# Selective-scan unit: states and output products in one group, B·C products beside the turning of x

## The chip, the cores and the metric

The kernel runs on one core of a Trainium2 chip. The metric is the device time of one execution in microseconds (us), lower is better. Of TensorE two names appear: PE is its matmul stream and PEld its weight loads. DVE is VectorE, ACT is ScalarE, and SP is the engine whose queue issues the DMAs.

## The reference, cut to what matters

One layer of a sequence model on 512 tokens, in float32. A state-space mixer (heads of 64 in 8 groups, state size 128) comes first, then further mixers and projections that the change doesn't touch. The part that matters is the scan:

```python
def step(state, inp):
    xc, ac, bc, cc = inp
    cs = jnp.cumsum(ac, axis=1)
    seg = cs[:, :, None] - cs[:, None, :]
    decay = jnp.exp(jnp.where(mask, seg, -jnp.inf))
    cb = jnp.einsum("blgn,bsgn->blsg", cc, bc)
    y_diag = jnp.einsum("blsg,blsgr,bsgrp->blgrp", cb, decay, xc)          # within the chunk
    y_off = jnp.einsum("blgn,bgrpn,blgr->blgrp", cc, state, jnp.exp(cs))   # from the state
    last = cs[:, -1]
    w_in = jnp.exp(last[:, None] - cs)
    new_state = state * jnp.exp(last)[..., None, None] + jnp.einsum("bsgn,bsgr,bsgrp->bgrpn", bc, w_in, xc)
    return new_state, y_diag + y_off
```

Around it stand the projections z, x, B, C = h @ w_in, a causal convolution with silu on x, B and C, and y = (y + d_skip·x)·silu(z). The kernel may cut the sequence into other chunks than the reference: it uses four chunks of 128 tokens.

## The kernel before

**GEMMs.** The projections are done by `gemm` (L178): 96 matmuls of 512 columns give two PSUM tiles (16 steps kt over the depth, for each two column blocks, and for each of those three products of split operands, L197 to L199). Weights come through `wchunk` (L160): one DMA of 512 KB, then `hi` on ACT (L171) and `lo` on DVE (L172).

**Groups, halves, units.** The loop runs over 8 groups g. A group has a GEMM for B and C, then for u = 0 and u = 1 a GEMM for x and one for z. One scan unit belongs to each half; they are called unit n = 2g + u here, 0 to 15. During the z GEMM of a half, `middle(kt)` puts the unit's steps between the GEMM's steps:

- kt 11, `ssd_pre`: a DMA that spreads the running decays over the partitions (`csr`, L1045, one buffer), eight transposes that turn x (`tp`, L1053), and on DVE `xdt` (L1056) and `xdw` (L1059).
- kt 12, `ssd_decay`: for each chunk on ACT the exponentials `dec` (L1097, L1099) and, but for chunk 0, `cex` (L1104); on DVE their products with `cbm` (L1100) and with C (L1105).
- kt 14, `ssd_states`: three products into `sa` and `sb` (L1073), then `st[0]` copied by ACT (L1079), and `st[1]`, `st[2]` each by a DVE multiply (L1081) of the state before and an add (L1083) of the new part.
- after the GEMM, `ssd_unit`: 28 matmuls with 64-row outputs into `yp`. Part 0 (L1122, 16 of them, within a chunk) reads `dec` and `xdt`; part 1 (L1124, 12 of them) reads `cex` and the state. The chunks run 3, 2, 1, 0 with the two parts in turn, so the first part 1 reads the last state, `st[2]`. Then DVE adds the skip (L1127), scales z (`zr`, L565), makes silu of it with ACT (`zt`, L566, L567) and multiplies (L573).

**B·C.** `bc_late` (L511) turns B (`btp`, L514; ACT copy `btok`, L515) and makes the products B·C (`cbp`, L518; masked by DVE to `cbm`, L520). It runs at kt 11 of the x GEMM of u = 0, a whole GEMM ahead of the unit that uses it. The tiles `tp`, `btp`, `cbp`, `sa`, `sb` share two PSUM buffers.

**Unit 0** has no z GEMM behind it yet: its `bc_late`, `ssd_pre`, `ssd_decay` and `ssd_states` stand at kt 1, 5, 6 and 9 of the x GEMM of u = 1. **Unit 15** is the last; after it PE goes on with the output projection, whose operand `ya` (ACT L596, DVE L597) is made of earlier outputs `y`, read back by DMA as `yst` (L606).

**What sets the order.** A scheduler gives each engine its instructions in one fixed order at build time; each engine then runs in that order and waits where an operand isn't there. `issue_after` keeps the 28 matmuls of a unit in their order. GEMM matmuls that don't depend on the unit can stand between them where the scheduler thinks it fit: seven do in unit 8 and ten in unit 15.

Of the kernel before, what the change touches and what calls it, by code (L numbers as in the profile page):

```python
# [13 lines left out]
P = 128  # L14
# [126 lines left out]
class _K:  # L141
    def __init__(self, tc, I, O, dbg):
        self.tc, self.nc, self.I, self.O, self.dbg = tc, tc.nc, I, O, dbg
        self.n = 0

    def nm(self, s):
        self.n += 1
# [30 lines left out]
    def gemm(self, chunks, acts, ncol=2, nk=4, tag=0, before=None, early=True, after=None):  # L178
        nc = self.nc
        ps = [self.pg.tile([P, S], F32, tag=f"g{j + tag}", name=self.nm("g")) for j in range(ncol)]  # L180
        self.mms = []
        nkt = len(chunks) * nk
        kt = 0
        width = ncol * P
        for src in chunks:
            if before:
                before(kt)
            hl = self.wchunk(src, width * nk, early=early)
            for k in range(nk):
                if after:  # L190
                    after(kt)
                a = acts[kt]
                hi, lo = hl[k * 2 // nk]
                for j in range(ncol):
                    o = k % (nk // 2) * width + j * P
                    c = slice(o, o + P)
                    nc.tensor.matmul(ps[j], hi[:, c], a[:, 0, :], start=kt == 0, stop=False)  # L197
                    nc.tensor.matmul(ps[j], hi[:, c], a[:, 1, :], start=False, stop=False)  # L198
                    mm = nc.tensor.matmul(ps[j], lo[:, c], a[:, 0, :], start=False, stop=kt == nkt - 1)  # L199
                    self.mms.append(mm.ins)  # L200
                kt += 1
        assert kt == nkt
        return ps
# [158 lines left out]
    def part1(self):  # L362
# [138 lines left out]
        for g in range(NG):  # L501

            ps = self.gemm(blk(g, 0), hn, after=middle) if g else ps_bc0
            prs = (None, None) if g else pr_bc0
            bt = self.conv_silu(ps[0], 32 + g, tmp.tile([P, S], F32, tag="B", name=f"B{g}", bufs=1), prs[0])
            ct = self.conv_silu(ps[1], 40 + g, tmp.tile([P, S], F32, tag="C", name=f"C{g}", bufs=1), prs[1])
            flush()
            btok = tmp.tile([P, 3, P], F32, tag="btok", name=f"btok{g}", bufs=1)
            cbm = tmp.tile([P, NC, P], F32, tag="cbm", name=f"cbm{g}", bufs=1)

            def bc_late(g=g, bt=bt, ct=ct, btok=btok, cbm=cbm):  # L511
                btp = self.pa.tile([P, NC, P], F32, tag="a", name=f"btp{g}")
                for c in range(3):
                    nc.tensor.transpose(btp[:, c, :], bt[:, c * P : c * P + P], self.ckc("ident"))  # L514
                nc.scalar.activation(btok, btp[:, 0:3, :], AF.Copy)  # L515
                cbp = self.pa.tile([P, NC, P], F32, tag="a", name=f"cbp{g}")
                for c in range(NC):
                    nc.tensor.matmul(cbp[:, c, :], bt[:, c * P : c * P + P], ct[:, c * P : c * P + P],  # L518
                                     start=True, stop=True)
                nc.vector.tensor_tensor(cbm, cbp, self.ckc("triu").unsqueeze(1).to_broadcast([P, NC, P]), ALU.mult)  # L520

            slow = None
            if g:
                mid[11] = [bc_late]
                self.ada(2)
            else:
                mid[11] = [dt_late]
            for u in range(2):  # L530
                if g == 0 and u == 1:
                    mid.update(slow)
                ps = self.gemm(blk(g, 1 + u), hn, after=middle) if g or u else ps_x0
                xs = []
                for j in range(2):
                    xs.append(self.conv_silu(ps[j], g * 4 + u * 2 + j,
                                             tmp.tile([P, S], F32, tag="xs", name=self.nm("xs"), bufs=4)))
                flush()
# [9 lines left out]
                steps = [lambda g=g, u=u, xs=xs, pre=pre: self.ssd_pre(g, u, xs, pre),  # L548
                         lambda g=g, u=u, ct=ct, cbm=cbm, pre=pre: self.ssd_decay(g, u, ct, cbm, pre),
                         lambda g=g, u=u, btok=btok, pre=pre: self.ssd_states(g, u, btok, pre)]  # L550
                unit = lambda g=g, u=u, xs=xs, pre=pre, yy=yg: self.ssd_unit(g, u, xs, pre, yy)
                if g or u:
                    mid.update({11: steps[0:1], 12: steps[1:2], 14: steps[2:3]})
                    late.append(unit)
                else:
                    slow = {1: [bc_late], 5: steps[0:1], 6: steps[1:2], 9: steps[2:3]}
                if g:
                    self.ada(3)
                ps = self.gemm(blk(g, 3 + u), hn, after=middle)
                flush()  # L560
                ths = []
                for j in range(2):
                    th = tmp.tile([P, S], F32, tag="th", name=self.nm("zt"))
                    zr = tmp.tile([P, S], F32, tag="pr", name=self.nm("zr"))
                    nc.vector.tensor_tensor(zr, ps[j], self.rb0, ALU.mult)  # L565
                    nc.scalar.activation(th, zr, AF.Tanh, scale=0.5)  # L566
                    nc.vector.scalar_tensor_tensor(th, th, 1.0, zr, ALU.add, ALU.mult)  # L567
                    ths.append(th)

                def gated(n=len(ys), yg=yg, ths=ths):  # L570
                    for j in range(2):
                        y = yg[j]
                        nc.vector.scalar_tensor_tensor(y, ths[j], 0.5, y, ALU.mult, ALU.mult)  # L573
                        self.sumsq(y)
                        if n + j < 16:
# [489 lines left out]
    def ssd_states(self, g, u, btok, pre):  # L1065
# [4 lines left out]
        sb = self.pa.tile([P, 1, 4, 64], F32, tag="a", name=self.nm("sb"))  # L1070
        parts = [sa[:, 0], sa[:, 1], sb[:, 0]]
        for c in range(3):
            nc.tensor.matmul(parts[c].rearrange("p h d -> p (h d)"), btok[:, c, :],  # L1073
                             xdw[:, c].rearrange("p h d -> p (h d)"), start=True, stop=True)
# [12 lines left out]

    def ssd_decay(self, g, u, ct, cbm, pre):
# [18 lines left out]
        pre.update(decs=decs, cexs=cexs)  # L1107


    def ssd_unit(self, g, u, xs, pre, yg):  # L1110
        nc, tc = self.nc, self.tc
        xdt, st = pre["xdt"], pre["st"]
        yp = [self.py.tile([P, S], F32, tag="y", name=self.nm("yp")) for _ in range(2)]
        prev = None
        for c in (3, 2, 1, 0):
            cl = slice(c * P, c * P + P)
            for part in range(2 if c else 1):
                for h in range(4):
                    o = yp[h // 2][64 * (h % 2) : 64 * (h % 2) + 64, cl]
                    with tc.issue_after(prev) if prev is not None else nullcontext():  # L1120
                        if part == 0:
                            mm = nc.tensor.matmul(o, xdt[:, c, h, :], pre["decs"][c][:, h, :], start=True, stop=c == 0)  # L1122
                        else:
                            mm = nc.tensor.matmul(o, st[c - 1][:, h, :], pre["cexs"][c][:, h, :], start=False, stop=True)  # L1124
# [51 lines left out]
```

## Time and profile before

| | us |
|---|---|
| median of three runs | 2075.62 (2073.63 to 2075.88) |
| the profiled execution, own time | 2072.95 |
| its span, first to last instruction | 2071.2 |
| PE busy | 2049.6 (99%) |
| DVE busy | 1310.7 (63%) |
| ACT busy | 946.2 (46%) |

The mean granted TensorE clock was 0.998 of full speed. The profile is of one execution: the time of a row is when an instruction started on its engine, behind it how long it took, and a note in brackets is idle time ahead of it with what ended it. A row with xN is N instructions in a run. Starts of PE's matmuls are the better measure there, since they are pipelined and their ends are modelled.

### The profile page before, as it was taken

Reading aid. Unit: us, or ns where it says so; the run is one execution under the profiler, and the core shown is the slowest. Engines: PE = TensorE matmul, PEld = TensorE weight load, DVE = VectorE, ACT = ScalarE, POOL = GpSimd, SP = SyncE. Lnnn points to the kernel's source line nnn. Section 1 sums busy time; section 2 is a strip of 40 time slices with the busy share of each in tenths; the row PEclk is TensorE's granted clock in tenths of the full one; section 3 lists DMA queues with packets and bytes.
Section 4 is the critical chain, followed back from the end, with each engine's and each line's share of the span. In section 5 each row is a group of like instructions: output and inputs, shape, how many; then the busy total and the mean of one; then the engine's idle time right before and its main releaser. Section 6 shows DMA issues by size and latency. Waiting matters only on the chain.

```text
span 2071.2 us, 26925 instructions
## 1 busy us (share of the span) xinstructions
PE 2049.6 (99%) x10032; PEld 1695.7 (82%) x10032; DVE 1310.7 (63%) x2308; ACT 946.2 (46%) x1758; POOL 50.0 (2%) x35
## 2 busy tenths in 40 slices
PE   8999999999999999999999999989999999999999
PEld 7888888888878888888888888878888788888887
DVE  7777777686776868777643544476776444764333
ACT  7473444444344443434432433344577424763222
POOL 0000000000010000000000000000000000000000
PEclk9999999999999999999999999999999999999999
DMA  7344555545454554454533333234111233233442
GB/s 240 101 163 153 184 179 176 173 153 183 156 186 167 167 170 143 163 173 143 166 129 123 112 92 102 82 110 150 62 46 62 70 99 94 84 112 105 149 142 92
DMA packets 92627, 277.26 MB, mean 134 GB/s; under 512 B 9744, under 2 KB 19984, under 8 KB 90448
## 3 DMA queue, kind: packets, MB, share of 16 engines
q1 hardware_dynamic: 92208, 275.54, 40.8%
q8 instruction: 78, 1.28, 0.3%
q14 instruction: 53, 0.43, 0.1%
q10 hardware_dynamic: 288, 0.01, 0.0%
HBM read 262.80 MB, written 12.71 MB: 133 GB/s over the span
## 4 chain that ended last, share of the span: by engine, by line
PE 93%; DVE 3%; ACT 2%; DMA 1%; issue 1%; DVEq 0%; ACTq 0%
PE g L197 27%; PE g L198 27%; PE g L199 27%; PE yp L1122 1%; PE yp L1124 1%; PE op L879 1%; PE g L217 1%; DVE lo L172 1%; PE g L219 1%; PE g L218 1%; PE gt L265 1%; PE gt L266 1%; PE gt L264 1%; PE tp L1053 1%; PE sa L1073 1%
## 5 line engine op out<-in xcount | busy, mean ns | idle before, releaser
L172 DVE TENSOR_TENSOR lo<-raw,hi 128x512 fp32r<-128x512 f32 (+2 forms) x704 | 476.6, 677 | 549.8 <-ACT hi L171 547.7
L171 ACT ACTIVATE hi<-raw 128x512 fp32r<-128x512 f32 (+2 forms) x704 | 428.4, 609 | 864.6 <-PE g L198 803.0
L197 PE MATMUL g<-hn,hi 128*128 128x512 f32 x1216 | 480.0, 395 | 0.0
L199 PE MATMUL g<-hn,lo 128*128 128x512 f32 x1216 | 474.1, 390 | 0.0
L198 PE MATMUL g<-hn,hi 128*128 128x512 f32 x1216 | 473.9, 390 | 0.0
L197 PEld LDWEIGHTS g<-hn,hi 128*128 128x128 f32 x1216 | 228.3, 188 | 49.0 <-issue 2.6
L199 PEld LDWEIGHTS g<-hn,lo 128*128 128x128 f32 x1216 | 228.2, 188 | 47.7 <-issue 0.2
L198 PEld LDWEIGHTS g<-hn,hi 128*128 128x128 f32 x1216 | 228.4, 188 | 46.7 <-issue 0.2
L198 PE MATMUL g<-h,hi 128*128 128x512 f32 x512 | 200.5, 392 | 0.7 <-DVE h L687 0.6
L199 PE MATMUL g<-h,lo 128*128 128x512 f32 x512 | 199.7, 390 | 0.0
L198 PE MATMUL g<-ya,hi 128*128 128x512 f32 x512 | 199.4, 390 | 0.0
L197 PE MATMUL g<-ya,hi 128*128 128x512 f32 x512 | 199.4, 390 | 0.0
L199 PE MATMUL g<-ya,lo 128*128 128x512 f32 x512 | 199.4, 389 | 0.0
L197 PE MATMUL g<-h,hi 128*128 128x512 f32 x512 | 199.2, 392 | 0.0
L1150 DVE CUSTOM_DVE_ANT_0 adaw<-adaw,adac 128x1024 f32<-128x1024 f32 x96 | 115.6, 1221 | 19.2 <-DMA adaw<-in_wada 19.2
L198 PEld LDWEIGHTS g<-h,hi 128*128 128x128 f32 x512 | 96.2, 188 | 22.8 <-DVE h L687 3.2
L197 PEld LDWEIGHTS g<-h,hi 128*128 128x128 f32 x512 | 96.0, 188 | 20.4 <-ACT h L686 1.1
L199 PEld LDWEIGHTS g<-ya,lo 128*128 128x128 f32 x512 | 96.1, 188 | 20.1 <-DVE lo L172 0.2
L197 PEld LDWEIGHTS g<-ya,hi 128*128 128x128 f32 x512 | 96.1, 188 | 20.1 <-issue 0.2
L198 PEld LDWEIGHTS g<-ya,hi 128*128 128x128 f32 x512 | 96.1, 188 | 19.8 <-issue 0.2
L199 PEld LDWEIGHTS g<-h,lo 128*128 128x128 f32 x512 | 96.2, 188 | 19.6
L335 DVE SCALAR_TENSOR_TENSOR xc<-pr,cwh,xc 128x511 f32<-128x511 f32 (+1 forms) x144 | 101.9, 747 | 0.0
(365 smaller groups left out, 2637.4 us busy)
## 6 DMA issues: line engine op xcount, KB each, us to landing
raw<-in_win SPq DMA_DIRECT2D x216, 512.0 KB, 3.5
adaw<-in_wada SPq DMA_DIRECT2D x96, 512.0 KB, 4.6
raw<-in_wout SPq DMA_DIRECT2D x88, 512.0 KB, 3.5
csr<-csd SPq DMA_DIRECT2D x16, 1024.0 KB, 4.7
xT<-in_xT SPq DMA_DIRECT2D x16, 256.0 KB, 4.2
raw<-in_win SPq DMA_DIRECT2D x16, 256.0 KB, 3.3
ydram<-y SPq DMA_DIRECT2D x16, 256.0 KB, 2.1
yst<-ydram SPq DMA_DIRECT2D x8, 512.0 KB, 4.3
```

What stands on the lines that cost most here:

```text
L171: self.last_hi = nc.scalar.activation(hi, raw[:, i * h : i * h + h], AF.Copy).ins
L172: self.last_lo = nc.vector.tensor_tensor(lo, raw[:, i * h : i * h + h], hi.bitcast(F32), ALU.subtract).ins
L197: nc.tensor.matmul(ps[j], hi[:, c], a[:, 0, :], start=kt == 0, stop=False)
L198: nc.tensor.matmul(ps[j], hi[:, c], a[:, 1, :], start=False, stop=False)
L199: mm = nc.tensor.matmul(ps[j], lo[:, c], a[:, 0, :], start=False, stop=kt == nkt - 1)
L217: nc.tensor.matmul(ps[j], hi[:, o], a[:, 0, :], start=first, stop=False)
L218: nc.tensor.matmul(ps[j], hi[:, o], a[:, 1, :], start=False, stop=False)
L219: mm = nc.tensor.matmul(ps[j], lo[:, o], a[:, 0, :], start=False, stop=last)
L264: nc.tensor.matmul(ps[t], a[:, 0, ts], hi, start=k == 0, stop=False)
L265: nc.tensor.matmul(ps[t], a[:, 0, ts], lo, start=False, stop=False)
L335: nc.vector.scalar_tensor_tensor(xc[:, s:], ps[:, : S - s], w(k), xc[:, s:], ALU.mult, ALU.add)
L1150: nc.vector.tensor_tensor_reduce(out=raw, in0=raw, in1=self.cb, op0=ALU.mult, op1=ALU.add, scale=1.0, scalar=0.0, accum_out=self.macc[:, i ...
```

## The change

It moves `ssd_states` from kt 14 into `ssd_unit`, right ahead of the 28 output products, and orders these as part 0 of the chunks 3, 2, 1, 0 and then part 1 of the chunks 1, 2, 3. `st[1]`'s multiply reads the first part in PSUM in place of ACT's copy; the copy remains, since part 1 of chunk 1 reads it. `bc_late` moves to kt 11 of the z GEMM of u = 0, behind `ssd_pre`. A `fence` keeps the first step of the next GEMM behind the last output product. Unit 0 keeps its places but for the states.

```diff
@@ gemm
-                for j in range(ncol):
-                    ... (three matmuls)
+                with self.tc.issue_after(self.fence) if self.fence is not None and kt == 0 else nullcontext():
+                    for j in range(ncol):
...
+                self.fence = None
@@ run
             if g:
-                mid[11] = [bc_late]
                 self.ada(2)
...
-                         lambda g=g, u=u, btok=btok, pre=pre: self.ssd_states(g, u, btok, pre)]
...
-                    mid.update({11: steps[0:1], 12: steps[1:2], 14: steps[2:3]})
+                    mid.update({11: steps[0:1] if u else [steps[0], bc_late], 12: steps[1:2]})
                     late.append(unit)
                 else:
-                    slow = {1: [bc_late], 5: steps[0:1], 6: steps[1:2], 9: steps[2:3]}
+                    slow = {1: [bc_late], 5: steps[0:1], 6: steps[1:2]}
@@ ssd_states
-                    ns, st[-1], self.exl[:, c, h0 : h0 + 4].unsqueeze(2).to_broadcast([P, 4, 64]), ALU.mult)
+                    ns, st[-1] if c > 1 else parts[0], self.exl[:, c, h0 : h0 + 4].unsqueeze(2).to_broadcast([P, 4, 64]), ALU.mult)
...
-        pre["st"] = st
+        return st, mm.ins
@@ ssd_unit
-        prev = None
-        for c in (3, 2, 1, 0):
-            cl = slice(c * P, c * P + P)
-            for part in range(2 if c else 1):
+        st, prev = self.ssd_states(g, u, btok, pre)
+        for part, chunks in ((0, (3, 2, 1, 0)), (1, (1, 2, 3))):
+            for c in chunks:
+                cl = slice(c * P, c * P + P)
...
-                            mm = nc.tensor.matmul(o, xdt[:, c, h, :], pre["decs"][c][:, h, :], start=True, stop=c == 0)
+                            mm = nc.tensor.matmul(o, xdt[:, c, h, :], pre["decs"][c][:, h, :], start=c == 3, stop=False,
+                                                  skip_group_check=True)
...
+        self.fence = prev
```

Where this moves instructions is seen in the orders of three engines. First **DVE in unit 7**, whose states are `st_4510`, `st_4513` before and `st_4524`, `st_4527` after (the add of each is its second row); `zr`, `zt` and `lo` are other work, for z and for weights. Before:

```order
L172 TENSOR_TENSOR lo_4598<-raw_4591,hi_4597 128x512
L1081 TENSOR_TENSOR st_4510<-st_4508,exl 128x256
L1083 TENSOR_TENSOR st_4510<-st_4510,sa_4503 128x256
L1081 TENSOR_TENSOR st_4513<-st_4510,exl 128x256
L1083 TENSOR_TENSOR st_4513<-st_4513,sb_4504 128x256
L565 TENSOR_TENSOR zr_4561<-g_4322,rb_602 128x512
L565 TENSOR_TENSOR zr_4566<-g_4323,rb_602 128x512
L172 TENSOR_TENSOR lo_4628<-raw_4625,hi_4627 128x512
L567 SCALAR_TENSOR_TENSOR zt_4560<-zt_4560,zr_4561 128x512
```

The same place after:

```order
L173 TENSOR_TENSOR lo_4598<-raw_4591,hi_4597 128x512
L566 TENSOR_TENSOR zr_4561<-g_4322,rb_602 128x512
L566 TENSOR_TENSOR zr_4566<-g_4323,rb_602 128x512
L173 TENSOR_TENSOR lo_4628<-raw_4625,hi_4627 128x512
L568 SCALAR_TENSOR_TENSOR zt_4560<-zt_4560,zr_4561 128x512
L1082 TENSOR_TENSOR st_4524<-sa_4517,exl 128x256
L568 SCALAR_TENSOR_TENSOR zt_4565<-zt_4565,zr_4566 128x512
L1084 TENSOR_TENSOR st_4524<-st_4524,sa_4517 128x256
L1082 TENSOR_TENSOR st_4527<-st_4524,exl 128x256
L1084 TENSOR_TENSOR st_4527<-st_4527,sb_4518 128x256
```

The four state operations have moved behind `zr`, `zr`, `lo` and the first `zt`, with the second `zt` among them. In the even units they stand as multiply, `zr`, add, `zr`, multiply, `zt`, add, `zt`, and four `dec` products and a `lo` stand directly ahead of them, since `cbm` is made only here.

Second, **ACT in unit 0**, at the end of its exponentials. `dec_1013` and `cex_1020` are unit 0's chunk 3, `xc` and `xs` the convolution of the next x, `dec_1310` the first of unit 1, which reads unit 1's `csr_1276`. Before (the states' copy `st_1056` stands 12 rows ahead of these):

```order
L1097 ACTIVATE dec_1013<-csr_962,cs 128x128 x4
L1104 ACTIVATE cex_1020<-csr_962 128x512
L171 ACTIVATE hi_1216<-raw_1214 128x512
L1099 ACTIVATE dec_1013<-dec_1013 128x512
L332 ACTIVATE xc_1117<-pr_1118,cwh 128x512
L332 ACTIVATE xc_1127<-pr_1128,cwh 128x512
L1037 ACTIVATE xs_1116<-xc_1117 128x512
L1097 ACTIVATE dec_1310<-csr_1276,cs 128x128 x3
```

After:

```order
L1098 ACTIVATE dec_1013<-csr_962,cs 128x128 x2
L1105 ACTIVATE cex_1020<-csr_962 128x512
L1100 ACTIVATE dec_1013<-dec_1013 128x512
L335 ACTIVATE xc_1104<-pr_1105,cwh 128x512
L335 ACTIVATE xc_1114<-pr_1115,cwh 128x512
L1080 ACTIVATE st_1130<-sa_1125 128x256
L1098 ACTIVATE dec_1310<-csr_1276,cs 128x128
L1038 ACTIVATE xs_1103<-xc_1104 128x512
L1038 ACTIVATE xs_1113<-xc_1114 128x512
```

The copy `st_1130` now stands behind both `xc`, and both `xs` stand behind the first `dec_1310`. On DVE the add of `st[1]` stands behind the two products that finish `xs`, and the two operations of `st[2]` behind that.

Third, **DVE in unit 15**, with `ya` for the output projection. Before:

```order
L1083 TENSOR_TENSOR st_8698<-st_8698,sa_8691 128x256
L565 TENSOR_TENSOR zr_8754<-g_8511,rb_602 128x512
L1081 TENSOR_TENSOR st_8701<-st_8698,exl 128x256
L172 TENSOR_TENSOR lo_8849<-raw_8846,hi_8848 128x512
L1083 TENSOR_TENSOR st_8701<-st_8701,sb_8692 128x256
L567 SCALAR_TENSOR_TENSOR zt_8748<-zt_8748,zr_8749 128x512
L597 SCALAR_TENSOR_TENSOR ya_8882<-yst_8880,pkt,ya_8882 128x512
L597 SCALAR_TENSOR_TENSOR ya_8885<-yst_8880,pkt,ya_8885 128x512
```

After:

```order
L1084 TENSOR_TENSOR st_8712<-st_8712,sa_8705 128x256
L173 TENSOR_TENSOR lo_8849<-raw_8846,hi_8848 128x512
L1082 TENSOR_TENSOR st_8715<-st_8712,exl 128x256
L568 SCALAR_TENSOR_TENSOR zt_8753<-zt_8753,zr_8754 128x512
L598 SCALAR_TENSOR_TENSOR ya_8882<-yst_8880,pkt,ya_8882 128x512
L598 SCALAR_TENSOR_TENSOR ya_8885<-yst_8880,pkt,ya_8885 128x512
L598 SCALAR_TENSOR_TENSOR ya_8890<-yst_8888,pkt,ya_8890 128x512
L598 SCALAR_TENSOR_TENSOR ya_8893<-yst_8888,pkt,ya_8893 128x512
L1084 TENSOR_TENSOR st_8715<-st_8715,sb_8706 128x256
```

The last add of the state stood ahead of the four `ya` and stands behind them now.

On PE, in the even units from 2 on, `btp` (three) and `cbp` (four) stood together a GEMM ahead; now six GEMM matmuls stand between the last `tp` and `btp`, and three between `btp` and `cbp`. Units 8 and 15 have no GEMM matmul inside their 28 products any more; in unit 0 four transposes of unit 1's x stand ahead of its last four products.

## Rows read from the trace of the kernel before

**Rows 1.** The page of the profile: busy time of each engine (us, share of the span, instructions), and the chain of work that ended last, as shares of the span by engine.

```profile
PE 2049.6 (99%) x10032; PEld 1695.7 (82%) x10032; DVE 1310.7 (63%) x2308; ACT 946.2 (46%) x1758; POOL 50.0 (2%) x35
...
PE 93%; DVE 3%; ACT 2%; DMA 1%; issue 1%; DVEq 0%; ACTq 0%
```

**Rows 2.** The waits of PE: engine and line, what it waited for, us in total, times, the longest.

```profile
PE yp L1124 <- DVE st L1083: 3.3, 3, 2.0
PE sx L293 <- ACT q L646: 2.6, 1, 2.6
```

**Rows 3.** The timeline of PE at units 8 (its first part 1) and 15 (its first part 1, and the GEMM behind its products).

```profile
579.60 0.66 PE L1124 MATMUL yp<-cex,st 128*64 128x128 f32 x8 [1.97 <-DVE st L1083]
...
996.38 0.66 PE L1124 MATMUL yp<-cex,st 128*64 128x128 f32 x8 [1.13 <-DVE st L1083]
...
999.15 0.50 PE L198 MATMUL g<-ya,hi 128*128 128x512 f32 x1
```

**Rows 4.** The timeline of PE around unit 7 (g = 3, u = 1): start, us, engine, line, operation, output and inputs, shape, count. First the matmuls of its states, then the last GEMM matmul, the start and the end of its 28 products (counted as twice as many records, since an f32 matmul runs as two) and the GEMM that follows.

```profile
498.71 1.03 PE L1073 MATMUL sa<-xdw,btok 128*128 128x256 f32 x4
...
499.82 0.58 PE L197 MATMUL g<-hn,hi 128*128 128x512 f32 x1
500.24 0.40 PE L198 MATMUL g<-hn,hi 128*128 128x512 f32 x1
...
502.55 0.39 PE L199 MATMUL g<-hn,lo 128*128 128x512 f32 x1
502.87 0.66 PE L1122 MATMUL yp<-dec,xdt 128*64 128x128 f32 x8
...
503.81 0.61 PE L1122 MATMUL yp<-dec,xdt 128*64 128x128 f32 x8
...
505.56 0.61 PE L1122 MATMUL yp<-dec,xdt 128*64 128x128 f32 x8
506.10 0.50 PE L197 MATMUL g<-hn,hi 128*128 128x512 f32 x1
506.43 0.39 PE L198 MATMUL g<-hn,hi 128*128 128x512 f32 x1
```

**Rows 5.** The timeline of PE around unit 6 (g = 3, u = 0): the B and C products in the x GEMM, and later the turning of x in the z GEMM.

```profile
421.42 0.49 PE L514 MATMUL btp<-ckt,B 128*128 128x128 f32 x3
...
422.56 0.48 PE L197 MATMUL g<-hn,hi 128*128 128x512 f32 x1
...
444.44 1.03 PE L1053 MATMUL tp<-ckt,xs 128*128 128x128 f32 x8
445.23 0.48 PE L197 MATMUL g<-hn,hi 128*128 128x512 f32 x1
```

**Rows 6.** The timeline of DVE around unit 6: the second reader of the first `tp`, then the last work ahead of where the `dec` products stand in the order after.

```profile
446.07 0.68 DVE L1059 TENSOR_TENSOR xdw<-tp,dtw 128x512 f32<-128x512 f32 x1
...
451.51 0.69 DVE L172 TENSOR_TENSOR lo<-raw,hi 128x512 fp32r<-128x512 f32 x1
```

**Rows 7.** The timeline of DVE around unit 7.

```profile
500.74 0.69 DVE L172 TENSOR_TENSOR lo<-raw,hi 128x512 fp32r<-128x512 f32 x1
501.34 0.42 DVE L1081 TENSOR_TENSOR st<-st,exl 128x256 f32<-128x256 f32 x1
501.86 0.42 DVE L1083 TENSOR_TENSOR st<-st,sa 128x256 f32<-128x256 f32 x1
...
503.19 1.28 DVE L565 TENSOR_TENSOR zr<-g,rb 128x512 f32<-128x512 f32 x2
```

**Rows 8.** The timeline of ACT around unit 7: the copy of the first state.

```profile
499.78 0.39 ACT L1079 ACTIVATE st<-sa 128x256 f32<-128x256 f32 x1 [0.47 <-PE sa L1073]
```

**Rows 9.** The timeline of PE at unit 0: the start of its products.

```profile
112.66 0.66 PE L1122 MATMUL yp<-dec,xdt 128*64 128x128 f32 x8
```

**Rows 10.** The timeline of DVE at unit 0: the `dec` product of chunk 3.

```profile
111.92 0.68 DVE L1100 TENSOR_TENSOR dec<-dec,cbm 128x512 f32<-128x512 f32 x1
```

**Rows 11.** The timeline of ACT at unit 0.

```profile
110.06 0.62 ACT L1104 ACTIVATE cex<-csr 128x512 f32<-128x512 f32 x1
110.58 0.62 ACT L171 ACTIVATE hi<-raw 128x512 fp32r<-128x512 f32 x1
111.11 0.62 ACT L1099 ACTIVATE dec<-dec 128x512 f32<-128x512 f32 x1
...
115.41 0.63 ACT L1037 ACTIVATE xs<-xc 128x512 f32<-128x512 f32 x1 [0.68 <-DVE xc L335]
117.09 0.99 ACT L1097 ACTIVATE dec<-csr,cs 128x128 f32<-128x128 f32 x3 [1.05 <-DMA csr<-csd]
```

**Rows 12.** The timeline of the DMAs that SP issues, at unit 0: the `csr` of unit 1.

```profile
110.70 0.33 SPq L1045 DMA_DIRECT2D csr<-csd  x1
```

**Rows 13.** The page of the profile, DMA issues: line, engine, operation, count, KB each, median us from issue to landing.

```profile
csr<-csd SPq DMA_DIRECT2D x16, 1024.0 KB, 4.7
```

**Rows 14.** The timeline of ACT at unit 15: four `ya`.

```profile
996.92 2.63 ACT L596 ACTIVATE ya<-yst,pkt 128x512 fp32r<-128x512 f32 x4 [1.13 <-DMA yst<-ydram]
```

**Rows 15.** A stretch of the span, inside the attention phase behind the scan's output projection, us from its start, length, then busy time (and instructions) of PE, PEld, DVE, ACT and POOL, the granted clock of PE, the DMAs' share and GB/s.

```profile
1356.00:1360.00 4.00, 3.86 (x17) 3.71 (x18) 1.78 (x3) 0.99 (x2) 0.00 (x0) 0.50 0.00 0
```

**Rows 16.** The timeline of PE at the program's start.

```profile
8.44 0.63 PE L218 MATMUL g<-hn,hi 128*128 128x512 f32 x1
8.87 0.57 PE L219 MATMUL g<-hn,lo 128*128 128x512 f32 x1
```

More of the change, by code (lines that the diff above doesn't have):

```diff
@@ L193, in gemm @@
                 hi, lo = hl[k * 2 // nk]
-                for j in range(ncol):
[L195 to L200, printed above, removed]
+                with self.tc.issue_after(self.fence) if self.fence is not None and kt == 0 else nullcontext():
+                    for j in range(ncol):
+                        o = k % (nk // 2) * width + j * P
+                        c = slice(o, o + P)
+                        nc.tensor.matmul(ps[j], hi[:, c], a[:, 0, :], start=kt == 0, stop=False)
+                        nc.tensor.matmul(ps[j], hi[:, c], a[:, 1, :], start=False, stop=False)
+                        mm = nc.tensor.matmul(ps[j], lo[:, c], a[:, 0, :], start=False, stop=kt == nkt - 1)
+                        self.mms.append(mm.ins)
+                self.fence = None
                 kt += 1
@@ L548, in part1 @@
                 steps = [lambda g=g, u=u, xs=xs, pre=pre: self.ssd_pre(g, u, xs, pre),
-                         lambda g=g, u=u, ct=ct, cbm=cbm, pre=pre: self.ssd_decay(g, u, ct, cbm, pre),
-                         lambda g=g, u=u, btok=btok, pre=pre: self.ssd_states(g, u, btok, pre)]
-                unit = lambda g=g, u=u, xs=xs, pre=pre, yy=yg: self.ssd_unit(g, u, xs, pre, yy)
+                         lambda g=g, u=u, ct=ct, cbm=cbm, pre=pre: self.ssd_decay(g, u, ct, cbm, pre)]
+                unit = lambda g=g, u=u, xs=xs, btok=btok, pre=pre, yy=yg: self.ssd_unit(g, u, xs, btok, pre, yy)
                 if g or u:
-                    mid.update({11: steps[0:1], 12: steps[1:2], 14: steps[2:3]})
+                    mid.update({11: steps[0:1] if u else [steps[0], bc_late], 12: steps[1:2]})
                     late.append(unit)
                 else:
-                    slow = {1: [bc_late], 5: steps[0:1], 6: steps[1:2], 9: steps[2:3]}
+                    slow = {1: [bc_late], 5: steps[0:1], 6: steps[1:2]}
                 if g:
@@ L1072, in ssd_states @@
         for c in range(3):
-            nc.tensor.matmul(parts[c].rearrange("p h d -> p (h d)"), btok[:, c, :],
-                             xdw[:, c].rearrange("p h d -> p (h d)"), start=True, stop=True)
+            mm = nc.tensor.matmul(parts[c].rearrange("p h d -> p (h d)"), btok[:, c, :],
+                                  xdw[:, c].rearrange("p h d -> p (h d)"), start=True, stop=True)
         st = []
@@ L1107, in ssd_decay, with ssd_unit @@
         pre.update(decs=decs, cexs=cexs)
-    def ssd_unit(self, g, u, xs, pre, yg):
+    def ssd_unit(self, g, u, xs, btok, pre, yg):
         nc, tc = self.nc, self.tc
-        xdt, st = pre["xdt"], pre["st"]
+        xdt = pre["xdt"]
         yp = [self.py.tile([P, S], F32, tag="y", name=self.nm("yp")) for _ in range(2)]
-        prev = None
-        for c in (3, 2, 1, 0):
-            cl = slice(c * P, c * P + P)
-            for part in range(2 if c else 1):
+        st, prev = self.ssd_states(g, u, btok, pre)
+        for part, chunks in ((0, (3, 2, 1, 0)), (1, (1, 2, 3))):
+            for c in chunks:
+                cl = slice(c * P, c * P + P)
                 for h in range(4):
                     o = yp[h // 2][64 * (h % 2) : 64 * (h % 2) + 64, cl]
-                    with tc.issue_after(prev) if prev is not None else nullcontext():
+                    with tc.issue_after(prev):
                         if part == 0:
-                            mm = nc.tensor.matmul(o, xdt[:, c, h, :], pre["decs"][c][:, h, :], start=True, stop=c == 0)
-                        else:
-                            mm = nc.tensor.matmul(o, st[c - 1][:, h, :], pre["cexs"][c][:, h, :], start=False, stop=True)
+                            mm = nc.tensor.matmul(o, xdt[:, c, h, :], pre["decs"][c][:, h, :], start=c == 3, stop=False,
+                                                  skip_group_check=True)
+                        else:
+                            mm = nc.tensor.matmul(o, st[c - 1][:, h, :], pre["cexs"][c][:, h, :], start=False,
+                                                  stop=c == 3, skip_group_check=True)
                     prev = mm.ins
+        self.fence = prev
         for j in range(2):
```

## The prediction

> **What bounds the kernel now.** I read the page first. PE is busy 99% of the span and carries 93% of the chain that ended last [rows 1]: 21 us of the 2071.2 are all that a change of order can give back, and any time for which PE stands is paid in full. Next came PE's waits: what this change aims at, output products that wait for the state, is 3.3 us in three places [rows 2], of which 1.97 lie in unit 8 and 1.13 in unit 15 [rows 3]. So there is little to win. The question is what the new order makes PE wait for, and that is read from the timelines of DVE and ACT around single units, with the new order of instructions laid over the old durations. "Needed" and "ready" below are times on the old clock of the trace.
>
> **Prices.** GEMM matmuls start 0.227 us apart. The states' group starts at 498.71, GEMM follows at 499.82 and is back in step at 500.24 [rows 4]: 1.11 + (0.42 − 0.23) + about 0.04, or 1.35; six records at 0.213 would be 1.28, so the group's two boundaries cost 0.07. The products start at 502.87, GEMM is back at 506.10 and 506.43: 0.09 late at the start, 3.23 for the group, 0.10 behind it, 3.42 in all; a quarter of the work takes (505.56 − 503.81)/4 = 0.437 per four matmuls [rows 4], so seven of these are 3.06, and this group's boundaries and starts cost about 0.4.
>
> **Merging states and products.** It saves one pair of boundaries in each of 16 units. Bounds: 0.07 (the states' group) and 0.4 (the products' group). I take 0.07, since it is the states' group whose boundaries go: −1.1 us; the other end would be −6.4.
>
> There is a rule on this. The Trainium skill, "TensorEngine Tiling (Array Packing)", Tiling Modes, says that a change of tiling mode drains the engine. The states are 128 wide, the products 64, so by it the drain remains where states meet products, and merging saves nothing there: the sum would be 1.1 us higher by it. The row's 0.07 stands with it more than with 0.4.
>
> **B·C products beside the turning of x.** They don't become one group with it. In seven even units (2 to 14) six GEMM matmuls stand behind `tp`, then `btp`, three more, `cbp`. Before, `btp` and `cbp` were one group, 421.42 to 422.56 [rows 5]. Split, it has one more pair of boundaries, 0.07 to 0.4; I take 0.13. And `btp` needs the PSUM buffer of the first `tp`: PE arrives at 445.23 + 6 × 0.23 = 446.6 [rows 5], the second reader ends at 446.07 + 0.68 = 446.75 [rows 6]: 0.1 to 0.15 of wait. Together +0.28 in each.
>
> **A new wait in the odd units.** The cover is gone. Before, 16 GEMM matmuls, over 3 us, lay between the states and their first reader; now only part 0 does, 16 products or 1.75 us. In unit 7 the states start at 502.87 − 0.1 − 1.35 = 501.42. DVE's order is lo, zr, zr, lo, zt, multiply, zt, add, multiply, add. From lo at 500.74 it steps 0.60 (lo at 500.74, next at 501.34; zr is 1.28 for two) [rows 7]: zr at 501.34, lo at 502.55, zt at 503.15, first multiply at 503.75, zt at 504.09, add at 504.69, multiply at 505.15, last add at 505.68, done 506.10 (a multiply that depends on the add steps 0.46, an add 0.52, as 501.34 to 501.86 [rows 7]). ACT's copy (0.39 [rows 8]) stands behind its two tanh and ends at about 503.6, just in time. PE has done part 0 and two chunks of part 1, 24 matmuls, at 502.77 + 6 × 0.437 = 505.4. It then waits **0.7 us**. Seven odd units (1 to 13): 7 × (0.7 − 0.07) = +4.4, less the 0.2 that is left of the old waits: +4.2.
>
> **And in the even units.** DVE: `dec` products first (below), then multiply, zr, add, zr, multiply, zt, add. Unit 6's states start at 444.44 + 0.8 for `tp` [rows 5] + 30 GEMM matmuls (6.8) + 1.4 for `btp` and `cbp` + 0.3 of wait and boundaries, or 453.8; with the multiply at 455.35 the same steps put the last add's end at 458.6 (the zt waits for a tanh that ACT gives behind three exponentials of the next unit, and those wait for PE's part 0), while PE gets there at 457.9: again 0.7. Units 2, 4, 6, 10, 12, 14: 6 × (0.7 + 0.28 − 0.07) = +5.5. The four `dec` products are now late as well, since `cbm` is: five operations from 451.51 [rows 6] at 0.61 end at 454.6, needed at 453.8 + 1.35 = 455.1. A slack of 0.5, no cost, but no more than that.
>
> **Unit 8.** It has the `adac` work on DVE and a wait of 1.97 before [rows 3]. In the new order one `zt` more (0.6) stands ahead of the last add and seven GEMM matmuls no longer fill the group, while part 0 is now done meanwhile: 0 to 1.0, I take +0.5, its B·C split included.
>
> **Unit 0.** This and unit 15 are the long ones. The new order has nine GEMM matmuls (2.04 us) fewer ahead of the unit, so PE could start the products at 112.66 − 0.1 − 2.04 = 110.5 [rows 9]. But the `dec` product of chunk 3 ended at 111.92 + 0.68 = 112.6 [rows 10], and in the new order at about 112.4, as its `hi` goes ahead of its first half: 1.9 of wait. Then `st[1]`. Its add stands on DVE behind the two products that finish `xs`; these wait for ACT's `xs`, and ACT's `xs` now stands behind the first `dec` of unit 1, which waits for that unit's `csr`. Before, that DMA went out at 110.70, when the last `cex` was read (110.06 + 0.62), and was waited for until 117.09, 6.4 us later [rows 11, 12]; `xs` ran at 115.41, ahead of it. Now it goes out at 111.1 and lands at 117.5; `dec` 0.4, two `xs` on ACT 1.1, the second `xs` on DVE 0.7, add 0.42: chunk 2 of part 1 starts at 120.1, chunk 3 a multiply and an add later at 121.1, and GEMM comes back at 121.7. Without waits it would be 110.5 + 3.5 = 114.1. That is **+7.6**; with the median landing of 4.7 [rows 13] in place of 6.4 it is +5.9. I take the row of this very transfer.
>
> **Unit 15.** The last add is now behind four `ya`. ACT makes these from 996.92, when the DMA landed, to 999.55 [rows 14]; DVE's fourth ends 0.75 later at 1000.3, the add at 1000.7, four products bring GEMM back at 1001.3. Before it was back at 999.15 [rows 3] with ten GEMM matmuls done inside the group (2.27), so at 996.9 by the same count: **+4.4**.
>
> **The clock.** In both PE stands for five us and more in one piece. In the trace the granted clock was 0.50 (1.2 GHz) between 1356 and 1360 [rows 15], where PE had stood 2.6 us [rows 2] and run single-column matmuls. At the program's start the matmuls are 0.43 apart (8.44, 8.87 [rows 16]), nine of them, in place of 0.227: 9 × 0.2 = 1.8 per fall. Bounds 0 (it doesn't fall) and 2.4; I take 1.8 at both: +3.6.
>
> **The sum.** Odd +4.2, even +5.5, unit 8 +0.5, unit 0 +7.6 − 0.1, unit 15 +4.4 − 0.1, clock +3.6: +25.6. On the profiled execution's own time, 2072.95 (its span 2071.2 with 1.75 around it), this is 2098.6; on the median 2075.62 it is 2101.2. The profiled execution lies at the lower end of the three; I say **2100**.
>
> **Rivals.**
> - *Only the small waits.* The long chains at units 0 and 15 come out short, since engines reach those points in another order in time (the `csr` lands in 4.7, `yst` earlier) and the clock stays up. Then +10.2 from the other units and some 5 from these two: 2090. For it: the landing differs from one transfer to the next, median 4.7. Against it: the fixed orders of ACT and DVE make these waits certain, only their length isn't.
> - *The decay products come too late in the even units.* The slack of 0.5 is used up by one `lo` that waits for its `hi`, or a late `adaw`, and PE waits at its first product too, for 1 us or more in six units: +6, with longer state chains and another fall of the clock at unit 8, +4: 2110. For it: five DVE operations without a gap in between. Against it: the same DVE ran such stretches without waits before.
> - *Faster.* The states' chain on DVE ends inside part 0's cover, which it does if the last add ends before the 24th product, 505.4 in unit 7, so 0.7 earlier than I make it, and the chains at units 0 and 15 are short. Then the merged groups give 1.1 to 6.4 and the old waits 3.3 go: 2069, at best 2066. Against it: DVE's order has zr, lo and zt ahead of the chain in all units, and each is 0.6.
> - *No change.* As this one, but with waits of 0.2 to 0.3 that cancel the gains: 2075.
>
> That the change doesn't do what it says is part of the forecast: `btp` and `cbp` are beside the turning of x, but not in its group.
>
> **How the numbers follow.** Forecast 0.62 (2095 to 2106), only the small waits 0.17, late decay products 0.11, faster 0.05, no change 0.05. The range leaves out the last two and the outer half of the second and third: 2086 to 2111. The lower end is 2100 with unit 0 at 5.9, unit 8 at 0, no fall of the clock, and half the per-unit waits (−1.7 − 0.5 − 3.6 − 5.6 = −11.4); some more from merging leads to 2086. A measurement of this kernel can tell about 0.2%, or 4.2 us, from no change: faster 0.05, within 0.05, slower 0.90.
>
> **What would show it.** PE's waits should list part 1 waiting for DVE's `st` add (L1084) in nearly all units, for 0.5 to 1 us each; at unit 0 part 0 waits about 2 us for `dec` and part 1 over 5 for `st`, with ACT waiting for `csr` just before; at unit 15 part 1 waits over 4 us for `st` with the `ya` of DVE in front. Behind both, matmuls 0.43 apart. `btp` should wait about 0.1 for `xdw`. I am wrong if part 1 starts without waits in most units, or if unit 0's `xs` doesn't wait for `csr`.

## The result and the profile after

The changed kernel takes 2099.82 us in the median of four runs (2098.88 to 2101.32), the kernel before 2075.75 beside it. The ratio is 1.0118, its 95% interval 1.0106 to 1.0131: slower by 24 us. The forecast was 2100. The profiled execution took 2098.88, its span is 2097.1, 25.9 more than that of before.

The page and the waits of PE, where the second view gives engine, line, what was waited for, us in total, times and the longest:

```profile
PE 2058.0 (98%) x10032; PEld 1697.1 (81%) x10032; DVE 1309.2 (62%) x2308; ACT 944.8 (45%) x1758; POOL 47.2 (2%) x35
...
PE 90%; DVE 6%; ACT 2%; DMA 1%; issue 1%; DVEq 0%; ACTq 0%; SPq 0%
```

```profile
PE yp L1126 <- DVE st L1084: 17.1, 19, 4.2
...
PE yp L1123 <- DVE dec L1101: 2.1, 1, 2.1
```

The chain has 90% PE in place of 93% and 6% DVE in place of 3% [rows 1]. Waits of part 1 for the state were 3.3 us in three places [rows 2]; now they are 17.1 in nineteen, and part 0 of one unit waits 2.1 for its decay product.

**Unit 7**, on PE and on DVE, which answers to [rows 4] and [rows 7]:

```profile
514.16 1.03 PE L1074 MATMUL sa<-xdw,btok 128*128 128x256 f32 x4
...
515.55 1.97 PE L1123 MATMUL yp<-dec,xdt 128*64 128x128 f32 x32
...
518.26 0.66 PE L1126 MATMUL yp<-cex,st 128*64 128x128 f32 x8 [0.31 <-DVE st L1084]
519.25 0.66 PE L1126 MATMUL yp<-cex,st 128*64 128x128 f32 x8 [0.33 <-DVE st L1084]
```

```profile
514.46 1.28 DVE L566 TENSOR_TENSOR zr<-g,rb 128x512 f32<-128x512 f32 x2
515.66 0.68 DVE L173 TENSOR_TENSOR lo<-raw,hi 128x512 fp32r<-128x512 f32 x1
516.26 0.68 DVE L568 SCALAR_TENSOR_TENSOR zt<-zt,zr 128x512 f32<-128x512 f32 x1
516.86 0.41 DVE L1082 TENSOR_TENSOR st<-sa,exl 128x256 f32<-128x256 f32 x1
517.20 0.68 DVE L568 SCALAR_TENSOR_TENSOR zt<-zt,zr 128x512 f32<-128x512 f32 x1
517.80 0.41 DVE L1084 TENSOR_TENSOR st<-st,sa 128x256 f32<-128x256 f32 x1
518.24 0.42 DVE L1082 TENSOR_TENSOR st<-st,exl 128x256 f32<-128x256 f32 x1
518.77 0.42 DVE L1084 TENSOR_TENSOR st<-st,sb 128x256 f32<-128x256 f32 x1
```

Between the first state product (514.16) and the first state multiply (516.86) DVE does zr, zr, lo and zt, 2.4 us that belong to other work. PE waits at chunk 2 until `st[1]` ends (518.21) and at chunk 3 until `st[2]` ends (519.19). Counted from where the pitch of the GEMM matmuls breaks to where it is back, the group delays the GEMM by 5.80 us; the two groups of before delayed it by 1.35 + 3.46 = 4.81.

**Unit 0**, ACT, the DMA issue, DVE and then PE, each in order of time, answering to [rows 9] to [rows 12]:

```profile
115.90 0.40 ACT L1098 ACTIVATE dec<-csr,cs 128x128 f32<-128x128 f32 x1 [2.52 <-DMA csr<-csd]
116.26 1.21 ACT L1038 ACTIVATE xs<-xc 128x512 f32<-128x512 f32 x2
```

```profile
111.21 0.33 SPq L1046 DMA_DIRECT2D csr<-csd  x1
```

```profile
112.09 0.69 DVE L1101 TENSOR_TENSOR dec<-dec,cbm 128x512 f32<-128x512 f32 x1
112.70 4.04 DVE L338 SCALAR_TENSOR_TENSOR xc<-pr,cwh,xc 128x511 f32<-128x511 f32 x6
116.66 0.42 DVE L1082 TENSOR_TENSOR st<-sa,exl 128x256 f32<-128x256 f32 x1
116.99 1.28 DVE L1039 SCALAR_TENSOR_TENSOR xs<-xs,xc 128x512 f32<-128x512 f32 x2
118.19 0.41 DVE L1084 TENSOR_TENSOR st<-st,sa 128x256 f32<-128x256 f32 x1
```

```profile
112.83 1.97 PE L1123 MATMUL yp<-dec,xdt 128*64 128x128 f32 x32 [2.06 <-DVE dec L1101]
114.63 0.61 PE L1126 MATMUL yp<-cex,st 128*64 128x128 f32 x8
118.66 0.69 PE L1126 MATMUL yp<-cex,st 128*64 128x128 f32 x8 [3.42 <-DVE st L1084]
119.29 1.12 PE L1054 MATMUL tp<-ckt,xs 128*128 128x128 f32 x4
120.33 1.12 PE L1126 MATMUL yp<-cex,st 128*64 128x128 f32 x8
121.39 0.80 PE L199 MATMUL g<-hn,hi 128*128 128x512 f32 x1
```

The next unit's `csr` goes out at 111.21. ACT stands 2.52 us for it and goes on at 115.90, then makes `xs`; DVE finishes `xs` and adds the state, and PE waits through all of it. But DVE is not idle meanwhile. From the `dec` product at 112.09 to the add at 118.19 it works without a gap: six operations of the convolution (`xc`, 4.04 us) stand ahead of the state's multiply, and the two `xs` ahead of the add. So in this execution it was DVE's own queue, more than the `csr`, that set when the add could run. Behind the wait PE is slow: the four transposes and the last four products take 1.04 and 1.06 us, and the granted clock from 119.3 to 122.3 was 0.50.

**Unit 15**, ACT, DVE and PE [rows 3, 14], and the granted clock of a stretch behind its wait (length, busy time and count of PE, PEld, DVE, ACT, POOL, then the clock, DMA share and GB/s):

```profile
1015.99 2.66 ACT L597 ACTIVATE ya<-yst,pkt 128x512 fp32r<-128x512 f32 x4 [1.08 <-DMA yst<-ydram]
```

```profile
1016.74 2.74 DVE L598 SCALAR_TENSOR_TENSOR ya<-yst,pkt,ya 128x512 fp32r<-128x512 f32 x4 [0.17 <-ACT ya L597]
1019.40 0.41 DVE L1084 TENSOR_TENSOR st<-st,sb 128x256 f32<-128x256 f32 x1
```

```profile
1014.98 0.66 PE L1126 MATMUL yp<-cex,st 128*64 128x128 f32 x8 [2.52 <-DVE st L1084]
1019.87 1.12 PE L1126 MATMUL yp<-cex,st 128*64 128x128 f32 x8 [4.23 <-DVE st L1084]
...
1021.51 0.63 PE L200 MATMUL g<-ya,hi 128*128 128x512 f32 x1
1021.93 0.63 PE L201 MATMUL g<-ya,lo 128*128 128x512 f32 x1
```

```profile
1018.00:1022.00 4.00, 2.13 (x11) 1.62 (x12) 3.70 (x10) 0.65 (x2) 0.00 (x0) 0.50 0.56 180
```

The last state add stands behind four `ya` of DVE, and these wait for those of ACT, which has its `yst` only at 1015.99. PE stands 2.52 us at chunk 2 and 4.23 at chunk 3, and then runs at a granted clock of 0.50, that is 1.2 GHz: matmuls 0.42 us apart.

**Where the 25.9 us are.** For each group of small matmuls I took the time by which the GEMM matmuls behind it start later than at their 0.227 us pitch, at the first of them and until the pitch is back:

| | forecast | before | after | difference |
|---|---|---|---|---|
| seven odd units (1 to 13) | +4.2 | 34.3 | 38.6 | +4.3 |
| six even units, B·C included | +5.5 | 36.9 | 43.1 | +6.3 |
| unit 8, B·C included | +0.5 | 8.5 | 8.2 | −0.2 |
| unit 0, with its clock (unit 1's transposes taken off) | +9.3 | 4.8 | 12.4 | +7.6 |
| unit 15, with its clock | +6.1 | 6.4 | 13.7 | +7.3 |
| all other places, by difference | 0 | | | +0.6 |
| together | 25.6 | | | 25.9 |

### The profile page after: what moved, and what is told of

Read it like the earlier page. It is cut to its first block, busy times and chain, and to the rows that moved or that the text cites. A ratio compares the mean times of both kernels' runs of the same rounds, so it can differ in the third digit from the quotient of the medians.

```text
span 2097.1 us, 26928 instructions
## 1 busy us (share of the span) xinstructions
PE 2058.0 (98%) x10032; PEld 1697.1 (81%) x10032; DVE 1309.2 (62%) x2308; ACT 944.8 (45%) x1758; POOL 47.2 (2%) x35
## 4 chain that ended last, share of the span: by engine, by line
PE 90%; DVE 6%; ACT 2%; DMA 1%; issue 1%; DVEq 0%; ACTq 0%; SPq 0%
PE g L199 26%; PE g L200 26%; PE g L201 26%; DVE lo L173 1%; PE op L880 1%; PE g L220 1%; PE g L222 1%; PE g L221 1%; PE gt L268 1%; PE gt L269 1%; DVE zr L566 1%; PE gt L267 1%; DMA adaw<-in_wada 1%; PE yp L1126 1%; DVE st L1082 1%
## 5 line engine op out<-in xcount | busy, mean ns | idle before, releaser
L338 DVE SCALAR_TENSOR_TENSOR xc<-pr,cwh,xc 128x511 f32<-128x511 f32 (+2 forms) x144 | 101.5, 746 | 0.0
```

Source lines behind the costliest of these rows:

```text
L338: nc.vector.scalar_tensor_tensor(xc[:, s:], ps[:, : S - s], w(k), xc[:, s:], ALU.mult, ALU.add)
```

## The experiments

The theory was that PE waits for a state chain that DVE and ACT run behind other work, directly ahead of its readers. The rivals: that the late B·C, the part order, the fence or the boundaries of the merged group cost the time, or that the chain is too long for its cover whatever its place.

**States back at their place.** `states_early`:

```diff
-                    mid.update({11: steps[0:1] if u else [steps[0], bc_late], 12: steps[1:2]})
+                    mid.update({11: steps[0:1] if u else [steps[0], bc_late], 12: steps[1:2], 14: steps[2:3]})
...
-                    slow = {1: [bc_late], 5: steps[0:1], 6: steps[1:2]}
+                    slow = {1: [bc_late], 5: steps[0:1], 6: steps[1:2], 9: steps[2:3]}
...
-        st, prev = self.ssd_states(g, u, btok, pre)
+        st, prev = pre["st"]
```

> The changed kernel with the three state products and their state chain back at kt 14 of the GEMM (kt 9 for unit 0); part order, fence and B C beside the turning of x stay. Theory (the loss is output products that wait for a state chain placed behind them): the waits on st vanish in all units, the split of B C (0.47 in seven units, 3.3) and unit 0's 2 us for its late decay product stay, the old waits of 3.3 to 5 go: 2075 to 2079. Rival (the part order, the fence or the late B C cost the time): it stays at 2090 or more.

2078.58 (ratio to before 1.0015, interval 1.0006 to 1.0025), as expected but for one wait for the state. Its waits of products are two:

```profile
PE yp L1124 <- DVE dec L1102: 2.0, 1, 2.0
...
PE yp L1127 <- DVE st L1085: 1.7, 1, 1.7
```

21 of the 24 us go with the place of the states. What is left is the split B·C, unit 0's late decay product and 1.7 in unit 15. The part order, the fence and the late B·C by themselves are not the loss.

**B·C back in the x GEMM.** `bc_early`:

```diff
             if g:
+                mid[11] = [bc_late]
                 self.ada(2)
...
-                    mid.update({11: steps[0:1] if u else [steps[0], bc_late], 12: steps[1:2]})
+                    mid.update({11: steps[0:1], 12: steps[1:2]})
```

> The changed kernel with B C back in the x GEMM, as one group. Theory: only the split group and its wait go, 7 x 0.47 = 3.3, the even units then wait for st like the odd ones, 0.6 to 0.8 each, and unit 0 and unit 15 stay: 2095 to 2098. Rival (B C beside the turning of x makes cbm, the decay products and with them the state chain late, and this is most of the loss): 2085 or less.

2101.08 (1.0122, 1.0106 to 1.0137): nothing gained, which neither the theory nor the rival had expected. The split goes as it should, 1.72 to 1.25 in seven units, 3.3 in all; the even units still wait for the state. Unit 8 takes it back in the profiled execution: with B·C the early way its group is 9.68 us (8.37 and 1.31 until the pitch is back) against 6.51, since all three chunks of part 1 wait there; unit 0 lost 1.0 more, to the clock (see the last section). The three waits:

```profile
593.16 0.66 PE L1127 MATMUL yp<-cex,st 128*64 128x128 f32 x8 [0.69 <-ACT st L1081]
594.62 0.66 PE L1127 MATMUL yp<-cex,st 128*64 128x128 f32 x8 [0.81 <-DVE st L1085]
596.49 1.06 PE L1127 MATMUL yp<-cex,st 128*64 128x128 f32 x8 [1.21 <-DVE st L1085]
```

The rival, that late B·C makes most of the loss, falls with it.

In unit 0, whose order this edit leaves alone, the run answers what the `csr` was worth:

```profile
113.42 0.68 DVE L1102 TENSOR_TENSOR dec<-dec,cbm 128x512 f32<-128x512 f32 x1
...
119.52 0.42 DVE L1085 TENSOR_TENSOR st<-st,sa 128x256 f32<-128x256 f32 x1
```

```profile
116.84 0.40 ACT L1099 ACTIVATE dec<-csr,cs 128x128 f32<-128x128 f32 x1 [2.14 <-DVE xc L338]
```

ACT goes on with unit 1's `dec` 3.42 us behind the start of the last `dec` product (113.42), where it was 3.81 in the changed kernel, yet the add starts 6.10 us behind that product in both. The earlier `csr` bought nothing, because DVE is busy throughout.

**The chain ahead of other work in units 0 and 15.** `chain_first_in_0_15`; in the order of instructions nothing else moves:

```diff
-            if c == 0:
+            with self.tc.high_priority():
+              if c == 0:
                 nc.scalar.activation(ns, parts[0], AF.Copy)
-            else:
+              else:
```

> The changed kernel with the state chain's ACT copy, multiplies and adds at high priority in the scheduler. In the order this moves them only in unit 0 (ahead of the next x's convolution and of the decay that waits for csr) and in unit 15 (ahead of the four ya); the other units stay as they are. Theory (two long chains and the clock behind them are half of the loss): unit 0 loses 5 of its 7.5 and unit 15 about 5 of 7.3, with one to two us of low clock: 2086 to 2090. Rival (the many small waits carry nearly all, and the two units' time comes back elsewhere, since the csr and ya must be waited for anyway): 2096 or more.

2092.04 (1.0080, 1.0067 to 1.0094), 8 less than the changed kernel where 10 to 14 were expected. Unit 0 is as expected, 12.4 to 6.6. Unit 15 falls only from 13.7 to 11.7: the four `ya` are behind the chain now, but other `ya`, both zr, a lo and the zt still stand in front of it or within it, and PE waits 2.11 and 1.82. And in unit 8, where nothing moved, the profiled execution lost 1.6 more to the clock. The low clock behind unit 15 also cost 0.8 more (its pitch is back after 2.25 us in place of 1.42). The first stretch here is of this kernel, the second of the changed one, both at unit 8:

```profile
589.38 0.66 PE L1127 MATMUL yp<-cex,st 128*64 128x128 f32 x8 [1.21 <-DVE st L1085]
...
590.65 0.63 PE L201 MATMUL g<-hn,lo 128*128 128x512 f32 x1
591.07 0.63 PE L199 MATMUL g<-hn,hi 128*128 128x512 f32 x1
```

```profile
593.64 0.66 PE L1126 MATMUL yp<-cex,st 128*64 128x128 f32 x8 [1.21 <-DVE st L1084]
...
594.79 0.40 PE L201 MATMUL g<-hn,lo 128*128 128x512 f32 x1
595.03 0.40 PE L199 MATMUL g<-hn,hi 128*128 128x512 f32 x1
```

**The chain ahead of other work in all units.** `chain_first_all` adds to that:

```diff
-                    nc.vector.tensor_tensor(zr, ps[j], self.rb0, ALU.mult)
+                    with self.tc.issue_after(self.st_last) if self.st_last is not None else nullcontext():
+                        nc.vector.tensor_tensor(zr, ps[j], self.rb0, ALU.mult)
```

> As chain_first_in_0_15, and DVE's zr of each unit queued behind the last state add. In the order the four state operations now stand together in all units but 8, behind the weights' lo. States still in one group with the products, B C still beside the turning of x, fence kept. Theory (the many small waits are DVE's zr, zt in front of the chain): the last add ends about 3.4 us after the first state product, needed at 3.97, so the waits in 13 units (0.5 to 0.75 each) go; the split of B C (3.3) and unit 0's wait for its decay product (1.8) stay: 2077 to 2083. Rival (the cover by part 0 is too short for the chain in any order): 2088 or more.

2081.28 (1.0023, 1.0012 to 1.0034), 18.5 less than the changed kernel with states and products still in one group and B·C at its new place. Unit 7 on PE and on DVE:

```profile
504.74 1.03 PE L1076 MATMUL sa<-xdw,btok 128*128 128x256 f32 x4
...
506.13 1.97 PE L1126 MATMUL yp<-dec,xdt 128*64 128x128 f32 x32
507.92 1.48 PE L1129 MATMUL yp<-cex,st 128*64 128x128 f32 x24
```

```profile
506.22 0.42 DVE L1085 TENSOR_TENSOR st<-sa,exl 128x256 f32<-128x256 f32 x1 [0.16 <-ACT st L1083]
...
507.66 0.42 DVE L1087 TENSOR_TENSOR st<-st,sb 128x256 f32<-128x256 f32 x1
```

The last add ends 3.34 us after the first state product (3.4 expected), and the products run through. Part 0 is cover enough for the chain alone; it isn't for the chain with zr, zr, lo and zt in front. The rival of a cover too short falls for the 13 ordinary units. Waits of 4.8 us for the state are left, all in units 8 and 15. In unit 8 two operations of other work (`adaw`, 1.2 us each) stand within the chain now, PE waits 1.21 and 1.87, and with the low clock behind it the group is longer than in the changed kernel, 9.84 us against 6.51. Unit 15 falls to 6.9.

**The merging by itself.** `chain_first_bc_early` is `chain_first_all` with the edit of `bc_early`.

> As chain_first_all with B C back in the x GEMM: the merging of states and products alone, without waits. It prices the merged group. By my 0.07 per unit it is 1.1 less than the kernel before, its old waits of 3 to 5 gone too, with 1.8 of unit 0's decay wait and some at 8 and 15: 2073 to 2077. By the rule that a change of mode drains, nothing is saved by the merging: 1 more. Rival (each boundary of a group costs the 0.4 of the products): 2066 to 2070.

2079.66 in ten runs from 2075.35 to 2082.97 (1.0016, 1.0007 to 1.0025), above what I expected: unit 8 has waits of 2.02 and 1.83 here, and in the profiled execution a low clock behind them and behind unit 15. In the 13 ordinary units the merged group is 4.60 + 0.15 = 4.75 without a wait, in this kernel and in `chain_first_all`, where two groups are 4.81: merging saves 0.06 per unit, the 0.07 of the states' boundaries and not the 0.4 of the products'.

**Without the fence.** `no_fence`:

```diff
-        self.fence = prev
```

> The changed kernel without its fence: the scheduler puts GEMM matmuls between the products, 10 and 18 and 6 in unit 0, 17 in unit 15, 1 or 3 ahead of the last four in the others. Theory (PE only stands because nothing may fill the waits): units 0 and 15 lose 8 to 10 us of waits and low clock, the others swap a wait of 0.5 for a boundary of up to 0.4: 2086 to 2092. Rival (the fence is no cause, the filling matmuls wait too or cost as much in boundaries): 2096 or more.

2085.63 (1.0045, 1.0032 to 1.0059), just under the range expected and 14 less than the changed kernel. Of the waits for the state 4.5 us are left, in seven places. In unit 0 ten GEMM matmuls stand ahead of the products, and part 0 starts at 113.49 without a wait: the 2 us for the decay product were the fence's doing. So more than half of what the waits cost is there because the fence lets nothing fill them; the other 10 us over the kernel before remain without it.

**The part order alone, on the kernel before.** `part_order_only`, and the same with the chain at high priority, `part_order_chain_first`:

```diff
-        for c in (3, 2, 1, 0):
-            cl = slice(c * P, c * P + P)
-            for part in range(2 if c else 1):
+        for part, chunks in ((0, (3, 2, 1, 0)), (1, (1, 2, 3))):
+            for c in chunks:
+                cl = slice(c * P, c * P + P)
```

(with the start flag on chunk 3 of part 0 alone and the stop flag on chunk 3 of part 1).

> The kernel before with one thing of the change: part 0 of the chunks 3, 2, 1, 0 and then part 1 of 1, 2, 3. States at kt 14, B C in the x GEMM, no fence. Theory: st[2] is now read by the last four products in place of the second four, so the old waits go (1.97, 1.13 and some tenths): 2070 to 2073. Rival (the order of the parts itself costs, or GEMM matmuls would have filled those waits): 2075 to 2080.

2073.68 (0.9995, 0.9986 to 1.0004), at the upper edge or just above what I expected and no more than a measurement tells from no change. Of the 3.3 us of waits that were to go, 2.5 are left, 1.2 and 1.3 in units 8 and 15.

> As part_order_only, with the state chain at high priority, which moves it ahead of zr, ya and lo in units 8 and 15 alone. Theory: of its two waits left, 1.2 and 1.3, most goes: 2070.5 to 2073.5, under the kernel before by 1 to 4. Rival: the ya and weights that come later then make the GEMM behind wait, no gain over part_order_only: 2073 to 2075.

2071.71 in eleven runs (0.9980, 0.9971 to 0.9989): below both kernels, as expected. One wait of part 1 is left, 0.4 us in unit 8.

## Why the prediction was right

- **The bound.** PE, busy 99% of the span and 93% of the chain, had little to give back, and it paid the new waits: those of part 1 and part 0 grew from 3.3 to 19.2. Three slips in the prediction have no consequence: of the "16 GEMM matmuls" between unit 7's states and their first reader, twelve are GEMM matmuls and four are products of part 0; 110.5 + 3.5 in unit 0 is 114.0; and half of +4.2 and +5.5, for the lower end, is 4.9 in place of 5.6.
- **Odd units: +4.2 forecast, +4.3 measured.** The order on DVE was as laid out, and the last add in unit 7 ended 5.03 us after the first state product where 4.68 was worked out. I had all of the wait at chunk 3; in unit 7 half of it comes at chunk 2, in the others less or none. `chain_first_all` shows the cause: with zr behind the chain the wait is gone.
- **Even units: +5.5 forecast, +6.3 measured.** The wait is as forecast: a group of 5.47 against 4.75 without one, so 0.72 for 0.7. The split of B·C was mis-sized, 1.72 − 1.25 = 0.47 for 0.28, the boundary between its two parts and `btp`'s wait together. The decay products were ready, and the rival in which they come too late did not happen.
- **Unit 0: +9.3 with its clock, +7.6 measured, and the path was wrong in part.** ACT waits for `csr` ahead of `xs` as described, and part 1 waits for the state, but for 3.42 us and not for over 5. The prediction let DVE wait for ACT's `xs`, and so made the landing of `csr` the term that sets the end. It left out the six convolution operations of DVE, 4.04 us, ahead of the state's multiply. With these DVE had no gap, and an earlier `csr` changed nothing (`bc_early`). Without its clock the unit came out at about +5.9, the alternative end that the prediction gave for a landing in the median 4.7 us; that the two agree is luck, since the landing was not what held PE. Why this transfer took 6.3 us before is not settled. In the ten traces it took 6.3 to 7.9 in the four kernels in which a weight transfer issued 1.41 us ahead of it was still on its way, and 4.2 to 4.6 in the six others, but no run was made to separate the two.
- **Unit 15: +6.1 with its clock, +7.3 measured.** The four `ya` were ahead of the last add as described. ACT began them 7.3 us behind the unit's first state product (1008.66 to 1015.99), where the old times laid over the new order give 6.3 (992.07 − 0.1 − 1.35 to 996.92): 1.0 of the 1.2 missed. The wait comes in two pieces. I left out the 2.52 at chunk 2, where zr and lo of DVE stand behind earlier `ya`; as far as the order on DVE tells, chunk 3 would have waited that much longer without it.
- **Unit 8: +0.5 forecast, −0.2 measured.** Its wait fell from 1.97 to 1.21, since part 0 is done meanwhile.
- **The clock.** 1.8 for each fall was near for both, though PE stood for 3.42 and 4.23 us in one piece and not for five. Behind unit 15 the pitch is back after 1.42 us where 0.13 is usual, and the last four products take 1.05 where unit 7's take 0.58: some 1.8. Behind unit 0 the pitch is back after 0.69, but the four transposes and four products ahead of it, 1.04 and 1.06 us, ran slowly too; with 0.4 and 0.58 as their usual times that is some 1.7. These two sums are estimates from the starts of the matmuls. The upper bound of 2.4 has no row behind it.
- **Merging: −0.07 per unit forecast, −0.06 measured.** The rule of the Trainium skill, "TensorEngine Tiling (Array Packing)", Tiling Modes, that a change of mode drains the engine, doesn't contradict this: the change from 128 to 64 columns remains in the merged group, and the saving is next to nothing.

So the sum was right to 0.3 us, and that is luck: its terms missed by up to 1.7 each and cancelled. What carries the reading, state chains that stand behind other work on DVE and ACT, was shown by runs that take them away: in unit 0 by `chain_first_in_0_15`, in the ordinary units and in most of unit 15 by `chain_first_all`, in all units but for 1.7 us in unit 15 by `states_early`. Within unit 0 the prediction named the wrong link.

## What to carry to other kernels

A group of matmuls whose later members read what other engines make of its first members is safe only if that chain runs first on those engines; look in the order of instructions at what stands in front of it, and add up all of it, on each engine, against the cover. An engine that visibly waits for a transfer need not be the one that holds the rest up. Merging two groups was worth 0.06 us here, a wait within it 0.7 and up to 4. Putting the independent half of the products first is the cheap part of the idea: it gives cover without moving the producers. By itself it could not be told from no change; with the chain at high priority it was the version that won, by 0.2%.

## What had not been expected of the hardware

Whether the clock falls is not settled by the wait alone. In unit 0 the changed kernel and `bc_early` have the same order and the same wait of 2.06 us ahead of part 0, but part 0 took 1.97 us in the profiled execution of the one and 2.61 in that of the other, and the next four products 0.61 and 1.07:

```profile
114.16 2.61 PE L1124 MATMUL yp<-dec,xdt 128*64 128x128 f32 x32 [2.06 <-DVE dec L1102]
116.55 1.07 PE L1127 MATMUL yp<-cex,st 128*64 128x128 f32 x8
```

In `bc_early` the granted clock was 0.50 from 115.5 to 119; in the changed kernel it was 1.00 from 115 to 118.6. Behind the wait of 1.21 us in unit 8, PE ran its next matmuls 0.43 us apart in the profiled execution of `chain_first_in_0_15` and 0.23 apart in that of the changed kernel; but there the wait at the chunk before differs as well, 0.51 and 0.11. Behind the groups after which the clock was low, the pitch was back after 0.69 to 2.34 us, where 0.13 is usual, so a fall cost 0.6 to 2.2 us in the GEMM alone. The clock goes with the scatter of the runs: the ten of `chain_first_bc_early` spread by 7.6 us, and their mean granted clock goes from 0.998 at 2075.35 to 0.995 at 2082.97. The kernel before, with fewer such waits, spreads by 6.8 us in its 24 runs beside it (0.998 at 2073.42, 0.996 at 2080.24), so the new waits are not shown to add scatter.
